# Slice 0 in other pieces: G in one transfer, X in halves, slice 1's X on the other queue, half of the narrow part in front of part B

## The chip, the cores and the metric

The kernel runs on one core of a Trainium2 chip. Times are device microseconds of that core; a timed execution is some 1.7 us longer than the span that the profile shows.

## The reference

The kernel computes the gradient of a weight: a sum over 16 batches and 512 rows of the product of an input (1024 columns) and an output gradient (768 columns).

```python
batch, m, k, n = 16, 512, 1024, 768
grad_weight = np.einsum('bmk,bmn->kn', input, grad_output)   # float32 in and out
```

As the kernel sees it, 8192 rows are 64 slices of 128; X is a slice of the input (128 x 1024), G one of the gradient (128 x 768).

## The kernel before

Matmuls run in bf16 and add up in fp32. Each slice takes 12 matmuls of 512 columns: part A (X groups 0 to 3 against the first 512 columns of G), part B (X groups 4 to 7 against the same), and part N (the last 256 columns of G, two interleaved sets, against each half of X). The list `ORDER` says up to which slice each part is taken in which turn; an exclamation mark closes the running sums of a part, which then leave their banks (the eight places in which matmuls add up).

Slices 1 to 63 come through GpSimd's queue, which casts to bf16 on the way (X of slice 1 excepted). Slice 0 and X of slice 1 come as fp32 through the sync and scalar queues, and are cast by DVE (VectorE) and ACT (ScalarE). While they come, TensorE runs matmuls on ones, to have its clock up by then. In the profiles PE is TensorE, PEld its weight load, POOL GpSimd and SP the sync engine.

```python
nc.sync.dma_start(out=gf[:, 0:NA], in_=G[0:P, 0:NA])      # NA = 512: 2 KB rows
nc.scalar.dma_start(out=xf[0], in_=X[0:P, :])             # 4 KB rows
nc.sync.dma_start(out=gf[:, NA:N], in_=G[0:P, NA:N])      # 1 KB rows
nc.scalar.dma_start(out=xf[1], in_=X[P : 2 * P, :])
# ... warm-up matmuls; loads of slices 1 to 63 on gpsimd ...
round_by("DVE", g0, gf, 0, 256)
round_by("ACT", g0, gf, 256, NA)
round_by("DVE", xs[0], xf[0], 0, P)
round_by("ACT", xs[0], xf[0], 2 * P, 4 * P)
round_by("DVE", xs[0], xf[0], P, 2 * P)
round_by("DVE", xs[0], xf[0], 4 * P, 6 * P)
round_by("ACT", xs[0], xf[0], 6 * P, 8 * P)
```

At the end, sums and stores of parts A and B alternate; the narrow part has been turned and stored before.

## Time and profile before

| | before |
|---|---|
| time, first three runs | 175.96 us (175.85 to 175.99) |
| span of the profile | 174.3 us |
| TensorE busy | 97% of the span |
| first useful matmul | 5.32 us |
| first matmul on slice 1 | 8.06 us |
| last matmul starts | 171.25 us |

The last three instants are start times in the trace. In its DMA records each of the first four transfers has 128 packets, one per row, and 16 semaphore writes, taken here as one for each of the 16 DMA engines; a transfer has landed when the semaphore is complete. The records do not name the engine; where the prediction speaks of the earliest one, it goes by the earliest semaphore write of each transfer. From 5.32 us on, matmuls of 512 columns follow each other at 0.216 us without a hole, so every shift at the head comes out at the end.

### The profile page before, as it was taken

How to read it: one execution, taken by the hardware profiler on the slowest of the kernel's cores; microseconds unless marked ns; L12 is line 12 of the kernel's file. 1: busy time of each engine (PE TensorE's matmuls, PEld its weight loads, DVE VectorE, ACT ScalarE, POOL GpSimd, SP SyncE). 2: the span in 40 equal slices, each digit the busy share in tenths (PEclk: the TensorE clock that was granted, in tenths of full speed). 3: DMA queues.
4: the chain of work that ended last, by engine and by line, in shares of the span. 5: the costliest groups of instructions: out<-in, count | busy, mean ns of one | idle time of the engine just before them, and what ended most of it. 6: DMA issues, size and time to landing. Idle time of an engine off the chain costs nothing.

```text
span 174.3 us, 2013 instructions
## 1 busy us (share of the span) xinstructions
PE 169.9 (97%) x793; PEld 78.4 (45%) x808; DVE 61.3 (35%) x103; ACT 6.2 (4%) x12; POOL 66.7 (38%) x129
## 2 busy tenths in 40 slices
PE   8999999999999999999999999999999999999993
PEld 3444444444444444444444444444444444444463
DVE  0655582883940039300000662200560003931122
ACT  2640000000000000000000000000000000000000
POOL 7444434444444444444444444444274200000000
PEclk9999999999999999999999999999999999999999
DMA  5999999999999999999999999999999990085623
GB/s 192 276 208 209 207 209 208 208 208 209 207 208 209 207 208 210 207 209 209 206 209 208 208 210 207 207 209 208 207 209 209 207 202 11 0 190 160 170 86 120
DMA packets 25048, 33.35 MB, mean 191 GB/s; under 512 B 6480, under 2 KB 16592, under 8 KB 25040
## 3 DMA queue, kind: packets, MB, share of 16 engines
q0 software_dynamic: 18000, 28.65, 89.9%
q10 hardware_dynamic: 4448, 2.10, 4.7%
q1 hardware_dynamic: 2592, 2.49, 4.2%
q8 instruction: 6, 0.10, 0.2%
q14 instruction: 2, 0.02, 0.0%
HBM read 58.72 MB, written 3.15 MB: 355 GB/s over the span
## 4 chain that ended last, share of the span: by engine, by line
PE 97%; issue 0%; DVE 0%
PE bank L127 63%; PE bank L134 32%; PE bank L81 3%; DVE acc L118 0%
## 5 line engine op out<-in xcount | busy, mean ns | idle before, releaser
L127 PE MATMUL bank<-gt,xt 128*128 128x512 bf16 (+2 forms) x515 | 108.3, 367 | 0.5
L127 PEld LDWEIGHTS <-xt 128*128 128x128 bf16 x524 | 50.2, 98 | 57.2
L118 DVE TENSOR_TENSOR acc<-bank,acc 128x512 f32<-128x512 f32 (+2 forms) x62 | 37.9, 667 | 73.4 <-PE bank L127 72.9
L134 PE MATMUL bank<-xt,gt 128*128 128x512 bf16 x242 | 54.8, 379 | 0.3
L97 POOL DMA_DIRECT2D xt<-in_input_dram x62 | 33.1, 533 | 38.7 <-DMA xt<-in_input_dram 36.5
L92 POOL DMA_DIRECT2D gt<-in_grad_output_dram x63 | 33.8, 536 | 31.2 <-DMA gt<-in_grad_output_dram 24.9
L134 PEld LDWEIGHTS <-gt 128*128 128x128 bf16 x252 | 24.6, 98 | 29.7
L118 DVE TENSOR_TENSOR acct<-bank,acct 128x512 f32<-128x512 f32 x24 | 15.7, 682 | 30.0 <-PE bank L134 29.9
L81 PE MATMUL bank<-const-bfloat16-1.0 128*128 128x512 bf16 (+1 forms) x12 | 4.6, 574 | 0.8 <-PEq L263 0.8
L81 PEld LDWEIGHTS <-const-bfloat16-1.0 128*128 128x128 bf16 x12 | 1.6, 140 | 3.5 <-issue 3.5
L122 DVE COPY acc<-bank 128x512 f32<-128x512 f32 x4 | 2.7, 687 | 1.0 <-PE bank L127 1.0
L180 DVE STREAM_TRANSPOSE turned<-acct 128x512 f32<-128x512 f32 x4 | 2.9, 715 | 0.1
L127 PEld LDWEIGHTS <-x 128*128 128x128 bf16 x16 | 1.6, 98 | 1.9 <-DVE x L107 0.2
L107 DVE CAST g<-gf 128x256 bf16<-128x256 f32 x2 | 0.6, 290 | 4.7 <-DMA gf<-in_grad_output_dram 4.7
L124 ACT COPY acc<-bank 128x512 f32<-128x512 f32 x4 | 2.1, 589 | 1.3 <-PE bank L127 1.3
L127 PE MATMUL bank<-gt,x 128*128 128x512 bf16 x8 | 2.1, 379 | 0.0
L127 PE MATMUL bank<-g,x 128*128 128x512 bf16 x8 | 2.0, 398 | 0.0
L122 DVE COPY acct<-bank 128x512 f32<-128x512 f32 x2 | 1.3, 686 | 1.3 <-PE bank L134 1.3
L107 ACT CAST x<-xf 128x256 bf16<-128x256 f32 x4 | 1.4, 409 | 0.0
L107 ACT ACT_TABLE_LOAD x1 | 1.3, 1283 | 1.7 <-PEq L263 1.7
L124 ACT COPY acct<-bank 128x512 f32<-128x512 f32 x2 | 1.1, 588 | 1.5 <-PE bank L134 1.5
L107 DVE CAST x<-xf 128x256 bf16<-128x256 f32 (+1 forms) x5 | 1.0, 260 | 0.0
(8 smaller groups left out, 3.3 us busy)
## 6 DMA issues: line engine op xcount, KB each, us to landing
xt<-in_input_dram POOLq DMA_DIRECT2D x62, 256.0 KB, 8.5
gt<-in_grad_output_dram POOLq DMA_DIRECT2D x63, 192.0 KB, 8.5
out_dram<-acc SPq DMA_DIRECT2D x13, 128.0 KB, 2.7
xf<-in_input_dram ACTq DMA_DIRECT2D x2, 512.0 KB, 5.1
out_dram<-turned ACTq DMA_DIRECT2D x4, 256.0 KB, 3.4
gf<-in_grad_output_dram SPq DMA_DIRECT2D x1, 256.0 KB, 3.9
out_dram<-acc SPq DMA_DIRECT2D x1, 256.0 KB, 2.0
gf<-in_grad_output_dram SPq DMA_DIRECT2D x1, 128.0 KB, 4.7
```

The costliest lines, as they stand in the source:

```text
L81: nc.tensor.matmul(wps[:, 0:cols], ones, nc.const_aps.tensor(1.0, (P, cols), bf16), start=True, stop=True,)
L92: nc.gpsimd.dma_start(out=gt, in_=G[s * P : (s + 1) * P, :])
L97: nc.gpsimd.dma_start(out=xs[s], in_=X[s * P : (s + 1) * P, :])
L107: copy(out=dst[:, c0:c1], in_=src[:, c0:c1])
L118: nc.vector.tensor_add(out=dst, in0=src, in1=dst)
L122: nc.vector.tensor_copy(out=dst, in_=src)
L124: nc.scalar.copy(out=dst, in_=src)
L127: nc.tensor.matmul(bank, xs[s][:, k * P : (k + 1) * P], gwide[s][:, c0:c1], start=start, stop=stop)
L134: nc.tensor.matmul(bank, gnarrow[s].rearrange("p (r t) -> p t r", t=NT)[:, t], xs[s][:, h * NA : (h + 1) * NA], start=start, stop=stop,)
L180: nc.vector.transpose(out=turned[:, h * hb : (h + 1) * hb, :, t], in_=dst.rearrange("p (b r) -> p b r", r=SQ),)
```

## The change

The intent: the first matmuls need only the first half of slice 0's X, so bring it alone and start earlier; bring G in larger rows; while the second half is on its way, do two of the four narrow matmuls (`H1`) first. The warm-up is shortened to match.

```diff
-    "A1! B1 N1 B2! N2 A2 N3! ...
+    "A1! H1 B1 N1 B2! N2 A2 N3! ...
-WARMUP = [512] * 10 + [128] * 2
+WARMUP = [512] * 9 + [128] * 4
@@ loads
-    nc.sync.dma_start(out=gf[:, 0:NA], in_=G[0:P, 0:NA])
-    nc.scalar.dma_start(out=xf[0], in_=X[0:P, :])
-    nc.sync.dma_start(out=gf[:, NA:N], in_=G[0:P, NA:N])
-    nc.scalar.dma_start(out=xf[1], in_=X[P : 2 * P, :])
+    nc.sync.dma_start(out=gf, in_=G[0:P, :])
+    nc.scalar.dma_start(out=xf[0][:, 0:NA], in_=X[0:P, 0:NA])
+    nc.sync.dma_start(out=xf[1], in_=X[P : 2 * P, :])
+    nc.scalar.dma_start(out=xf[0][:, NA:K], in_=X[0:P, NA:K])
@@ casts
-    round_by("DVE", g0, gf, 0, 256)
-    round_by("ACT", g0, gf, 256, NA)
-    ... (x of slice 0 in five casts)
+    round_by("DVE", g0, gf, 0, 304)
+    round_by("ACT", g0, gf, 304, NA)
+    for k in range(0, KS // 2, 2):
+        round_by("DVE", xs[0], xf[0], k * P, (k + 1) * P)
+        round_by("ACT", xs[0], xf[0], (k + 1) * P, (k + 2) * P)
+    round_by("DVE", g0, gf, NA, N)
@@ behind the copies of banks 0 and 1
-            if s == 0 and i == 0:
-                round_by("DVE", g0, gf, NA, N)
+            if s == 0 and i == 1:
+                round_by("DVE", xs[0], xf[0], 4 * P, 6 * P)
+                round_by("ACT", xs[0], xf[0], 6 * P, 8 * P)
... (half_slice(), which opens two banks of part N ahead, and its bookkeeping)
```

More of the change, by code (lines that the diff above doesn't have):

```diff
@@ L17 @@
 ORDER = (
-    "A1! B1 N1 B2! N2 A2 N3! A3 B3 A4! B5 N5 B6! N7 A6 N8! A9! B10 N9 B12! N12! A12! "
+    "A1! H1 B1 N1 B2! N2 A2 N3! A3 B3 A4! B5 N5 B6! N7 A6 N8! A9! B10 N9 B12! N12! A12! "
     "B15 AB17! n17! AB26! n26! AB41! n41! AB47 A50! B50! N64!"
 ).split()
-WARMUP = [512] * 10 + [128] * 2
+WARMUP = [512] * 9 + [128] * 4
 XBUFS = 42
@@ L107, in round_by @@
         copy(out=dst[:, c0:c1], in_=src[:, c0:c1])
-    round_by("DVE", g0, gf, 0, 256)
-    round_by("ACT", g0, gf, 256, NA)
-    round_by("DVE", xs[0], xf[0], 0, P)
-    round_by("ACT", xs[0], xf[0], 2 * P, 4 * P)
-    round_by("DVE", xs[0], xf[0], P, 2 * P)
-    round_by("DVE", xs[0], xf[0], 4 * P, 6 * P)
-    round_by("ACT", xs[0], xf[0], 6 * P, 8 * P)
+    round_by("DVE", g0, gf, 0, 304)
[4 more added lines that the diff above has]
+    round_by("DVE", g0, gf, NA, N)
     def add_out(dst, src):
@@ L148, in __init__ @@
             self.first = True
+            self.ahead = 0
             self.banks = {}
@@ L196, in slice_by_slice, with half_slice @@
                 part.done += 1
-                first = not part.banks
-                for i in range(len(part.groups)):
+                ahead, part.ahead = part.ahead, 0
+                first = len(part.banks) == ahead
+                for i in range(ahead, len(part.groups)):
                     if first:
                         open_bank(part, i)
-                for i in range(len(part.groups)):
+                for i in range(ahead, len(part.groups)):
                     add_slice(part, i, s, first, close and s == upto - 1)
+    def half_slice(part):
+        part.ahead = len(part.groups) // 2
+        for i in range(part.ahead):
+            open_bank(part, i)
+            add_slice(part, i, part.done, True, False)
     def bank_by_bank(part, upto):
@@ L212 @@
     for i, step in enumerate(ORDER):
-        if i == 2:
+        if step == "H1":
+            half_slice(parts["N"])
+            continue
+        if i == 3:
             round_by("DVE", xs[1], xf[1], 4 * P, 6 * P)
```

## The prediction

> **What bounds the kernel now.** I read the engine shares and the chain that ended last on the page first, then the chain in order of time, then the timeline of the first 9 us on PE, PEld, DVE and ACT, then the issues with their time to landing.
>
> ```profile
> PE 169.9 (97%) x793; PEld 78.4 (45%) x808; DVE 61.3 (35%) x103; ACT 6.2 (4%) x12; POOL 66.7 (38%) x129
> ...
> PE 97%; issue 0%; DVE 0%
> PE bank L127 63%; PE bank L134 32%; PE bank L81 3%; DVE acc L118 0%
> ```
>
> TensorE is the chain. In order of time it has no hole:
>
> ```profile
> 0.78 4.64 PE bank L81 x12
> 5.42 1.95 PE bank L127 x8
> 7.36 0.86 PE bank L134 x4
> 8.22 0.86 PE bank L127 x4
> ...
> 164.76 6.72 PE bank L127 x58
> ```
>
> The warm-up (L81) runs to 5.4 us, then useful matmuls follow start to start at 0.216 us (0.86 us for 4) until 171.5 us; the last sums and stores follow to 174.3 us. (The 0.05 us "issue" entries in this chain lie where a matmul's record is missing: two starts 0.43 us apart, twice the usual step.) So only two things can move the time: when the first useful matmul starts, and whether a hole opens. The first 9 us:
>
> ```profile
> 4.71 0.41 ACT L107 CAST g<-gf 128x256 bf16<-128x256 f32 x1 [1.76 <-DMA gf<-in_grad_output_dram]
> 4.71 0.29 DVE L107 CAST g<-gf 128x256 bf16<-128x256 f32 x1 [4.71 <-DMA gf<-in_grad_output_dram]
> ...
> 5.32 1.55 PEld L127 LDWEIGHTS <-x 128*128 128x128 bf16 x8 [0.17 <-DVE x L107]
> 5.32 2.04 PE L127 MATMUL bank<-g,x 128*128 128x512 bf16 x8
> ...
> 7.20 1.03 PE L134 MATMUL bank<-x,g 128*128 128x512 bf16 x4
> 8.06 1.03 PE L127 MATMUL bank<-gt,x 128*128 128x512 bf16 x4
> ```
>
> The first useful matmul starts at 5.32 us, 0.17 us after PEld was free, released by DVE's cast of x (5.04 to 5.27). That cast waited for X of slice 0, which landed at 5.02 us; G's wide part had landed at 4.68. The page has the times to landing (median us at the line's end; the landing instants come from the same trace):
>
> ```profile
> xf<-in_input_dram ACTq DMA_DIRECT2D x2, 512.0 KB, 5.1
> ...
> gf<-in_grad_output_dram SPq DMA_DIRECT2D x1, 256.0 KB, 3.9
> ...
> gf<-in_grad_output_dram SPq DMA_DIRECT2D x1, 128.0 KB, 4.7
> ```
>
> **What the Trainium skill says.** "TensorE: Matmul & The Clock Gate", Part 1: the array starts at half clock, and sustained activity opens the gate after about 3.4 us of a free-running window; 512 columns take 426.7 ns cold and 215.7 ns warm. The trace agrees: warm-up matmuls are 0.427 us apart, later ones 0.216, and the clock record begins at 5.63 us, inside the first useful matmul. "DMA: Bandwidth & Descriptors", "Queues, rings and completion order": each DMA engine takes packets of its queues in turn, and the semaphore write of a transfer lands behind that engine's earlier writes. The trace's packet records agree: on an engine, 2 KB packets of G and 4 KB packets of X alternate one to one. Both points carry the prediction.
>
> **The change part by part.**
>
> *Packets.* Typical durations in the records are 46 ns for 1 KB, 84 for 2 KB, 159 for 4 KB; 3 KB is not there, and I estimate 122 by the midpoint of 84 and 159. Each of the 16 engines carries 8 packets of each of the four first transfers. The engines repeat one pattern, the last lagging the first by 0.62 us. On the earliest one, before: first X packet 2.34; semaphore of G's wide part 3.68, of X slice 0 3.99; narrow G starts 4.00, X slice 1 4.25, so a queue pauses 0.25 to 0.3 us after its semaphore; semaphores 4.80 and 5.74. Landing is the latest engine's semaphore plus 0.3 to 0.4 us.
>
> *First phase after.* At the first X packet five G packets are left. 5 x 122 + 8 x 84 = 1.28 us instead of 5 x 84 + 8 x 159 = 1.69 (measured 1.65). With 0.06 us for the longer G packets before it, X's first half has its semaphore at 2.40 + 1.28 = 3.68 (0.31 earlier) and G at about 3.51 (0.17 earlier). Landings: X half 5.02 - 0.31 = 4.71, whole G 4.68 - 0.17 = 4.51.
>
> *First matmul.* DVE casts 304 columns: 0.29 us for 256 and 0.22 for 128 give 0.32, so 4.53 to 4.85; consecutive casts overlap by some 0.08, so x of group 0 runs 4.77 to 4.99, and with 0.055 us of release the weight load is at 5.05. ACT's shorter g cast is done by 4.9. The new warm-up (nine 512s and four 128s) ends at 0.78 + 9 x 0.427 + 4 x 0.107 = 5.05 instead of 5.26, so it is in nobody's way. The start moves 5.32 to 5.05. Until 5.63 the clock is half, so 0.27 us of earlier start is worth half: matmuls start at 5.05, 5.47, 5.77, 5.99, then the two narrow ones at 6.20 and 6.42, ready for part B at 6.63 against 6.77 for the seventh matmul before. Gain so far 0.13 us.
>
> *What part B waits for.* Before, groups 4 to 7 of slice 0 were in the same X transfer. Now they are in the second half, which shares every engine with the 4 KB rows of slice 1. On the earliest engine X slice 1 can start at 3.51 + 0.25 = 3.76 and both need 8 x (159 + 84) ns = 1.94 us, the half coming last: semaphore 5.70, nearly the 5.74 that X slice 1 had before, since the bytes in front are the same (1408 KB). That one landed at 7.03; so the half lands at about 6.99. DVE's copy of bank 0 (5.7 to 6.4) is then over; the cast of groups 4 and 5 takes 0.29: 7.01 to 7.30, and with 0.055 the first B matmul starts at 7.36. TensorE idles 7.36 - 6.63 = 0.73 us. The two narrow matmuls moved in front cover 2 x 0.216 = 0.43 of what would have been 1.16.
>
> *Afterwards.* Six matmuls later, at 7.36 + 6 x 0.216 = 8.66, comes slice 1 of B, against 8.06: 0.60 us late. X of slice 1 (landing about 7) is cast by DVE and ACT after their bank copies by 8.1; G of slice 1 landed at 7.49 before and may slip 0.1 or 0.2. Slice 2 landed at 8.46 and 9.70 for matmuls at 10.65, slice 3 at 10.65 and 11.90 for 13.2. A later TensorE only widens these margins. The moved g cast and the 304/208 split lie beside waiting time and cost nothing. The tail is untouched.
>
> *Sum.* -0.13 + 0.73 = +0.60 us: 176.56.
>
> **The rivals.**
>
> *The half lands in time.* If the smaller packets get ahead of the 4 KB ones, or slice 1 starts late, the half lands by 6.2 and its cast follows the bank copy at 6.3 to 6.6: no hole, 175.83. For it: the cast was put exactly behind that copy, as if the data were known to be there, and the warm-up shortened by 0.21 us fits my new start. Against it: strict alternation in the records. For a half-way landing at 6.6 the hole is 0.33 and the time 176.16.
>
> *The start does not move.* If G in 3 KB rows lands later instead (the first packets are slow), the start stays at 5.3 and the hole is about 0.5: 176.5 as well, for the end of the hole is set by the half's landing and not by the start. In that case moving G is worth nothing.
>
> *A larger loss.* If the idle time delayed the clock, or three queues share the engines while the half is in flight (the GpSimd queue sends its first packet at 5.28), the half lands at 7.3 and the time is 176.9. A throttle for microseconds would take more idle than 0.7 us by the skill's window, and I give it little.
>
> **Range and chances.** The mechanical sum says 176.56; the tuned look of the change speaks for the first rival, at about one in four. Between them I take 176.4, with 175.8 to 176.9 as the range: the low end is the gain without a hole, the high end a landing at 7.3. The three times before span 0.14 us. Two per cent would be 3.5 us, several times anything above.
>
> **What would show it.** In the timeline: the first cast of g near 4.5 instead of 4.71, the first L127 matmul near 5.05 instead of 5.32; six matmuls without a hole; then a PEld or PE idle entry of about 0.7 us released by DVE's cast of x; the first matmul on gt near 8.66 instead of 8.06; after it the same sequence, shifted. In the waits: DVE for xf at 6.4 to 7.0. Wrong if the second half lands before 6.3, if the start moves by less than 0.1, or if holes open after 9 us.

## The result

The changed kernel takes 177.36 us (median of 6 runs, 177.34 to 177.51) against 176.04 (6 runs, 175.85 to 176.47). A ratio is the mean time of one kernel's fast runs over that of the other's of the same rounds, so not quite the ratio of these medians: 1.0075, interval 1.0062 to 1.0087. It is slower by 1.3 us, which is outside the range that I gave (175.8 to 176.9).

The chain that ended last, on the page of the changed kernel:

```profile
PE 93%; DMA 4%; issue 1%; DVE 0%; ACTq 0%
PE bank L127 62%; PE bank L134 31%; DMA xf<-in_input_dram 4%; ACTq L74 0%; DVE x L108 0%; DVE acc L118 0%
```

A DMA has entered a chain that was all TensorE, and the warm-up's 3% is gone from it. In order of time (start us, duration us, what):

```profile
1.18 6.49 DMA xf<-in_input_dram
7.70 0.30 DVE x L108
8.05 1.04 PE bank L127 x4
...
166.05 6.72 PE bank L127 x58
```

Everything up to 8.05 us now hangs on one transfer, issued at 1.18 us on the scalar queue: the second half of slice 0's X, landing at 7.67 us. The last entry is 1.29 us later than before. The timeline of the changed kernel (start us, duration us, engine, line, operation, in brackets idle time and releaser):

```profile
4.58 0.32 DVE L108 CAST g<-gf 128x304 bf16<-128x304 f32 x1 [4.58 <-DMA gf<-in_grad_output_dram]
...
5.23 1.78 PE L127 MATMUL bank<-g,x 128*128 128x512 bf16 x4
...
6.84 0.60 PE L134 MATMUL bank<-x,g 128*128 128x512 bf16 x2
...
7.70 0.29 DVE L108 CAST x<-xf 128x256 bf16<-128x256 f32 x1 [1.13 <-DMA xf<-in_input_dram]
...
8.04 0.55 PEld L127 LDWEIGHTS <-x 128*128 128x128 bf16 x4 [1.10 <-DVE x L108]
8.05 1.04 PE L127 MATMUL bank<-g,x 128*128 128x512 bf16 x4 [0.61 <-DVE x L108]
...
9.36 0.59 PE L127 MATMUL bank<-gt,x 128*128 128x512 bf16 x2
```

The start did move, from 5.32 to 5.23 us. The four matmuls of part A take 1.78 us because most of them ran at half clock (starts 0.40 to 0.43 us apart; the clock record shows full clock only from 6.77 us, against 5.63 before). The two narrow ones start at 6.84 and 7.06, so part B could have started at 7.06 + 0.216 = 7.28. It starts at 8.05: a hole of 0.77 us. (The bracket's 0.61 is shorter because a matmul's end is modelled later than the next could start.) Slice 1 begins at 9.36 instead of 8.06, 1.29 us late, and the last matmul starts at 172.54 instead of 171.25, also 1.29 late. So nothing happens after 9 us, and the whole loss is 7.28 - 6.77 = 0.51 us of later matmuls in front, plus the 0.77 us hole.

Who had the engines while the second half was due? The DMA view of the window from 4.4 to 5.2 us, first of the kernel before (queue, kind: packets, MB, share of 16 engines):

```profile
q10 hardware_dynamic: 68, 0.27, 82.3%
q1 hardware_dynamic: 90, 0.08, 28.6%
```

and of the changed kernel:

```profile
q1 hardware_dynamic: 53, 0.22, 71.0%
q10 hardware_dynamic: 35, 0.06, 20.6%
```

Queue 1 is sync, queue 10 scalar. In the changed kernel sync carries slice 1's X here, which nobody needs yet, and scalar the tail of the first half and the beginning of the second: 53 packets of 4 KB against 35, of which 31 are rows of 2 KB and 4 semaphore writes. My prediction counted on one to one. In the next 0.8 us, from 5.2 to 6.0, it is one to one:

```profile
q1 hardware_dynamic: 47, 0.19, 59.4%
q10 hardware_dynamic: 47, 0.10, 30.8%
```

So the second half loses its time at the start. By the packet records slice 1's X began at 4.12 us, 0.31 after the earliest semaphore write of its queue's G, and the second half at 4.61, 0.61 after that of the first half. Meanwhile the engines moved less: 320 GB/s from 3.8 to 4.6 us, against 397 in the kernel before.

### The profile page after: what moved, and what is told of

It reads as the page before. It is cut to its first block, busy times and chain, and to the rows that moved or that the text cites. A ratio compares the mean times of both kernels' runs of the same rounds, so it can differ in the third digit from the quotient of the medians.

```text
span 175.6 us, 2016 instructions
## 1 busy us (share of the span) xinstructions
PE 170.6 (97%) x794; PEld 78.5 (45%) x809; DVE 61.4 (35%) x103; ACT 6.4 (4%) x13; POOL 66.4 (38%) x129
## 3 DMA queue, kind: packets, MB, share of 16 engines
q1 hardware_dynamic: 2592, 3.02, 5.0%
## 4 chain that ended last, share of the span: by engine, by line
PE 93%; DMA 4%; issue 1%; DVE 0%; ACTq 0%
PE bank L127 62%; PE bank L134 31%; DMA xf<-in_input_dram 4%; ACTq L74 0%; DVE x L108 0%; DVE acc L118 0%
## 5 line engine op out<-in xcount | busy, mean ns | idle before, releaser
L127 PE MATMUL bank<-g,x 128*128 128x512 bf16 x8 | 2.8, 491 | 0.6 <-DVE x L108 0.6
L108 DVE CAST g<-gf 128x304 bf16<-128x304 f32 (+1 forms) x2 | 0.6, 302 | 4.6 <-DMA gf<-in_grad_output_dram 4.6
L108 ACT CAST x<-xf 128x256 bf16<-128x256 f32 (+1 forms) x5 | 1.6, 361 | 0.8 <-DMA xf<-in_input_dram 0.8
L134 PE MATMUL bank<-x,g 128*128 128x512 bf16 x4 | 1.2, 379 | 0.0
```

The lines of the kernel that those rows point to most:

```text
L108: copy(out=dst[:, c0:c1], in_=src[:, c0:c1])
L127: nc.tensor.matmul(bank, xs[s][:, k * P : (k + 1) * P], gwide[s][:, c0:c1], start=start, stop=stop)
L134: nc.tensor.matmul(bank, gnarrow[s].rearrange("p (r t) -> p t r", t=NT)[:, t], xs[s][:, h * NA : (h + 1) * NA], start=start, stop=stop,)
```

## The experiments

Landings below are those of the trace, counted from the start of the span. The diffs start from the changed kernel, except where one says "before". By the 2% rule x1_held counts as "unclear" and all others as "same"; what is read here is smaller than 2% and rests on the intervals and the traces, one trace for each kernel.

### Slice 1's X last (x1_last)

```diff
-    nc.sync.dma_start(out=xf[1], in_=X[P : 2 * P, :])
     nc.scalar.dma_start(out=xf[0][:, NA:K], in_=X[0:P, NA:K])
+    nc.scalar.dma_start(out=xf[1], in_=X[P : 2 * P, :])
```

> The changed kernel, with X of slice 1 moved from the sync queue to the scalar queue behind the second half of slice 0's X, so nothing of its size shares the engines with that half. Theory (the hole in front of part B lasts until the second half lands, and the half is late because slice 1's 4 KB rows share the engines): the half lands near 6.0 us instead of 7.67, the hole of 0.77 us closes, first matmul on G of slice 1 at 8.0 (clock open at 5.6) to 8.6 (clock open at 6.8) instead of 9.36; time 175.9 to 176.6. Rival (small 2 KB rows land late by themselves): the half still lands after 7.2, hole stays, 177.2 to 177.4.

176.81 us, ratio to before 1.0041 (1.0026 to 1.0055). The second half landed at 5.50 us, and part B started at 6.78 without a hole: the theory's mechanism holds. But the time is above its range. Slice 1's X now landed at 8.63, because GpSimd's first transfers went in front of it (G of slice 1 landed at 6.64 instead of 7.49). The timeline on PE:

```profile
6.78 1.04 PE L127 MATMUL bank<-g,x 128*128 128x512 bf16 x4
7.65 0.59 PE L134 MATMUL bank<-x,g 128*128 128x512 bf16 x2
9.01 1.04 PE L127 MATMUL bank<-gt,x 128*128 128x512 bf16 x4 [0.76 <-DVE x L108]
```

The hole has moved from in front of part B to in front of slice 1.

### Without the narrow half in front (no_h1)

```diff
-    "A1! H1 B1 N1 ...
+    "A1! B1 N1 ...
```

> The changed kernel without the half of the narrow part in front of part B (all four narrow matmuls of slice 0 behind B). Theory (part B's start is set by a landing, not by the matmuls in front): B starts at the same 8.05 us, and two more matmuls follow it, so 0.43 us longer, 177.8. Rival (the new order of matmuls itself costs, by banks or casts): the same 177.36 or less.

177.72 us, ratio 1.0091 (1.0075 to 1.0107). Part B started at 8.03, as with H1, and the hole grew; the four narrow matmuls behind it put slice 1 at 9.77 instead of 9.36, 0.41 us later. So H1 pays for itself with its two matmuls, and a landing sets the start of part B.

### A longer warm-up (warm_11)

```diff
-WARMUP = [512] * 9 + [128] * 4
+WARMUP = [512] * 11 + [128] * 2
```

> The changed kernel with a longer warm-up, eleven of 512 and two of 128 columns, so that the first useful matmul comes at about 5.7 us instead of 5.23. Theory (the hole in front of part B absorbs everything before it): the same time within 0.1 us, 177.3 to 177.5, with B still starting near 8.05. Rival (an early start or the clock's opening decides): 0.2 to 0.5 us longer, or shorter if the longer warm-up opens the clock earlier.

177.36 us, ratio 1.0072 (1.0058 to 1.0086), the same as the changed kernel. The first useful matmul came at 5.63 instead of 5.23, part B at 8.04. An earlier start, the main purpose of the change, is worth nothing while the hole is there; nor does the clock matter: it rose at 6.08 in no_h1, at 6.50 here and at 6.77 in the changed kernel, and part B starts at 8.03 to 8.05 in all three.

### X of slice 0 in one piece again (whole_x0)

```diff
-    nc.scalar.dma_start(out=xf[0][:, 0:NA], in_=X[0:P, 0:NA])
+    nc.scalar.dma_start(out=xf[0], in_=X[0:P, :])
-    nc.scalar.dma_start(out=xf[0][:, NA:K], in_=X[0:P, NA:K])
```

> The changed kernel with slice 0's X in one transfer of whole rows again, G in one transfer and X of slice 1 on the sync queue as changed. Theory (cutting X in halves puts slice 1's rows in front of the second half): X of slice 0 lands near 5.3 to 5.4, first matmul near 5.7, no hole; time 176.1 to 176.8, depending on when the clock opens. Rival (G in one transfer or slice 1 on the sync queue is what costs): 177.2 or more.

176.46 us, ratio 1.0022 (1.0008 to 1.0036). X landed at 5.38, the first matmul started at 5.71, no hole. Cutting X in halves is what makes the hole possible. What is left, some 0.4 us in the medians, fits the later start (5.71 against 5.32), for G in one piece delays X.

### G in two pieces again (g_split)

```diff
-    nc.sync.dma_start(out=gf, in_=G[0:P, :])
+    nc.sync.dma_start(out=gf[:, 0:NA], in_=G[0:P, 0:NA])
+    nc.sync.dma_start(out=gf[:, NA:N], in_=G[0:P, NA:N])
```

> The changed kernel with only G of slice 0 back in two transfers (wide, then narrow) on the sync queue, X of slice 1 behind them, X of slice 0 still in halves. Theory (X of slice 1 reaches the engines as soon as the whole G is through, just before the second half starts, and takes two packets for its one): now the 1 KB narrow rows stand in that place, the half lands at 5.6 to 6.3 us, no hole in front of part B; slice 1's X lands 7.2 to 7.7; time 175.9 to 176.5. Rival (any second half on the scalar queue is late while slice 1 shares the engines): half after 7.2, 177.0 or more.

177.37 us, ratio 1.0072 (1.0059 to 1.0084): the time missed the expectation, though the landing that it is about hit it. The second half landed at 5.40 with the narrow rows of G in the place of slice 1's X. Then slice 1's X landed at 8.44 instead of by 7.7, and slice 1 began at 8.82, 0.76 us late. The rest is at the end, and was not expected: from the start of the last matmul to the end of the span took 3.44 us instead of 3.03. With five transfers at the head instead of four, the rotation of the eight semaphores puts the last store on the first of them. The end of the program waits for the eight in a fixed order, 0.06 us each; here the other waits come after the last store has landed, where before they came while it was under way. I read this from the semaphore waits in the trace. No run was made for it alone, but x1_halves, also with five, has 3.45 us, and lead, with five and one store fewer, 3.02.

### The two second transfers exchanged (swap)

```diff
-    nc.sync.dma_start(out=xf[1], in_=X[P : 2 * P, :])
-    nc.scalar.dma_start(out=xf[0][:, NA:K], in_=X[0:P, NA:K])
+    nc.sync.dma_start(out=xf[0][:, NA:K], in_=X[0:P, NA:K])
+    nc.scalar.dma_start(out=xf[1], in_=X[P : 2 * P, :])
```

> The changed kernel with the two second transfers exchanged: second half of slice 0's X behind G on sync, X of slice 1 behind the first half on scalar. Theory (who starts second on the engines loses): the half lands at 6.6 to 7.0 instead of 7.67, part B starts 7.0 to 7.4 instead of 8.05, time 176.4 to 176.8. Rival (2 KB packets always lose two to one against 4 KB packets, whichever queue): half after 7.4, time 177.1 or more.

176.19 us, ratio 1.0008 (0.9996 to 1.0021): as fast as before, 0.2 us better than expected. The half landed at 6.27 and slice 1's X at 7.44; there is no hole. The DMA view of the same window as above, 4.4 to 5.2 us:

```profile
q10 hardware_dynamic: 51, 0.21, 65.8%
q1 hardware_dynamic: 66, 0.13, 42.2%
```

The half, now on queue 1, has the 66, so rows of 2 KB do not always lose to rows of 4 KB. The bytes are those of the changed kernel, and all of slice 1's X lands only 0.25 us later than there (7.19). The useful start at 5.00 us brought no gain in this trace, for its clock rose only at 6.78; slice 1 began at 8.47, and the profiled run is the slowest of the five (176.44).

### Slice 1's X in halves too (x1_halves)

```diff
-    nc.sync.dma_start(out=xf[1], in_=X[P : 2 * P, :])
+    nc.sync.dma_start(out=xf[1][:, NA:K], in_=X[P : 2 * P, NA:K])
     nc.scalar.dma_start(out=xf[0][:, NA:K], in_=X[0:P, NA:K])
+    nc.scalar.dma_start(out=xf[1][:, 0:NA], in_=X[P : 2 * P, 0:NA])
```

> The changed kernel with X of slice 1 in halves too: the half that part B needs first behind G on sync, the other behind slice 0's second half on scalar. Theory (the bytes that share the engines with slice 0's second half decide): 256 KB less in front, the half lands at 6.2 to 6.7, part B starts no later than 7.1 to 7.3, slice 1's last half lands at 7.3 to 7.8; time 176.0 to 176.6. Rival: as x1_last, a later landing takes the place of the first and the time stays near 176.8.

176.96 us, ratio 1.0058 (1.0045 to 1.0070), above the expectation. The second half landed at 6.88, part B started at 7.25, slice 1 at 8.56, 0.50 us late; the longer end adds 0.42. With 256 KB less in front, the half still came later than the 256 KB of slice 1 on the sync queue (6.27): fewer bytes help less than coming first.

### The short warm-up alone (b_warm9)

```diff
 before:
-WARMUP = [512] * 10 + [128] * 2
+WARMUP = [512] * 9 + [128] * 4
```

> The kernel before with nothing changed but the warm-up, nine of 512 and four of 128 columns. Theory (the clock opens at an instant that varies from run to run, and the first useful matmul waits for slice 0's X): the same as before within 0.2 us, 175.85 to 176.25, first matmul at 5.3. Rival (the shorter warm-up itself opens the clock a microsecond later, as in the changed kernel's trace): 0.3 to 0.5 us longer in every run.

175.98 us, ratio 1.0004 (0.9990 to 1.0017). The first matmul started at 5.28, and the clock was up at 3.78 us already. With the same nine-and-four warm-up the clock record began at 6.77 in the changed kernel's profile, 6.08 in no_h1 and 4.90 in x1_last. So the instant is not set by this warm-up; it varies from trace to trace.

### The sync queue held back by 0.2 us (g_late)

```diff
+    nc.vector.memset(gf[:, 0:64], 0.0)
     nc.sync.dma_start(out=gf, in_=G[0:P, :])
     ...
+    nc.vector.memset(xf[1][:, 0:64], 0.0)
     nc.sync.dma_start(out=xf[1], in_=X[P : 2 * P, :])
```

> The changed kernel with two small DVE memsets (64 columns of the tiles of G and of slice 1's X, overwritten by the transfers) that hold the sync queue back by some 0.2 us, so that the scalar queue starts first and its first half is through before G. Theory (of two queues, the one whose next transfer comes to the engines first is served first): slice 0's second half now comes first, lands 6.2 to 6.8 instead of 7.67, slice 1's X after it, part B starts by 7.2, time 176.2 to 176.8. Rival (the engines prefer the sync queue, whoever comes first): the half lands at 7.4 or later, time 177.1 or more.

Four runs: 176.06, 176.14, 176.38 and 177.38; median 176.26, ratio 1.0022, interval 0.9991 to 1.0054, so the time alone does not tell it from the kernel before. The trace tells more. G was issued at 0.96 instead of 0.74 us. The first half landed at 3.80 (4.92 in the changed kernel), the second at 5.52, slice 1's X at 7.37, and there is no hole. The window from 4.2 to 5.0 us:

```profile
q10 hardware_dynamic: 126, 0.23, 75.7%
q1 hardware_dynamic: 34, 0.10, 32.2%
```

The scalar queue, which had the smaller count in the changed kernel, has 126 packets against 34 (semaphore writes included). So it is not the sync queue that is preferred. The second half began at 4.06 us, slice 1's X only at 4.71, when three quarters of the half's packets had started: here the one that came first was mostly on its way before the other began. The run at 177.38 has the time of the changed kernel; that the order fell the other way there would fit, but it has no trace.

### What is needed next in front (lead)

```diff
-    nc.sync.dma_start(out=gf, in_=G[0:P, :])
+    nc.sync.dma_start(out=gf[:, 0:NA], in_=G[0:P, 0:NA])
     nc.scalar.dma_start(out=xf[0][:, 0:NA], in_=X[0:P, 0:NA])
-    nc.sync.dma_start(out=xf[1], in_=X[P : 2 * P, :])
-    nc.scalar.dma_start(out=xf[0][:, NA:K], in_=X[0:P, NA:K])
+    nc.sync.dma_start(out=xf[0][:, NA:K], in_=X[0:P, NA:K])
+    nc.sync.dma_start(out=gf[:, NA:N], in_=G[0:P, NA:N])
+    nc.scalar.dma_start(out=xf[1], in_=X[P : 2 * P, :])
... (no H1; warm-up 8 and 4; narrow cast behind X's; one store fewer)
```

> An attempt to beat both: only what a matmul group needs next is in front. Sync: wide G, second half of slice 0's X, narrow G; scalar: first half, X of slice 1; order of matmuls as before; warm-up eight of 512 and four of 128; one store fewer at the end, so that the number of transfers and with it the order of the final waits is as before. Theory: first half lands 4.2 to 4.4, first matmul near 4.7 instead of 5.3, second half 5.7 to 6.2, slice 1 by 7.5, no hole over 0.3 us; 175.7 to 176.1, the clock's instant deciding. Rival (what is put last lands late and opens a hole in its turn): slice 1 or narrow G after 8, time 176.4 or more.

177.41 us, ratio 1.0068 (1.0055 to 1.0080): a miss. The first half landed at 4.58, the second at 5.91, slice 1's X at 6.85, and the narrow part of G, last on its queue beside GpSimd's transfers, at 8.04. The timeline on PE:

```profile
4.89 2.63 PE L127 MATMUL bank<-g,x 128*128 128x512 bf16 x8
8.41 1.19 PE L134 MATMUL bank<-x,g 128*128 128x512 bf16 x4 [0.89 <-DVE g L109]
```

The rival came true: what is put last opens a hole of its own.

### Slice 1's X issued 2 us later (x1_held)

```diff
-    nc.sync.dma_start(out=xf[1], in_=X[P : 2 * P, :])
     nc.scalar.dma_start(out=xf[0][:, NA:K], in_=X[0:P, NA:K])
+    nc.scalar.copy(out=xf[1][:, 0:64], in_=nc.const_aps.tensor(1.0, (P, 64), bf16))
+    nc.sync.dma_start(out=xf[1], in_=X[P : 2 * P, :])
```

> The changed kernel with nothing moved but the instant at which slice 1's X is issued: a small ACT copy into its tile, after ACT's table load, holds that one transfer back from 1.2 to about 3.2 us. G, both halves and their queues stay. Theory (slice 1's X delays slice 0's second half only because it comes to the engines first): the second half lands at 5.5 to 6.3 instead of 7.67, slice 1's X at 7.3 to 8.0, no hole over 0.3 us in front of part B; time 175.8 to 176.4. Rival (G in one transfer, or the half's own queue, makes it late): half after 7, time 177.0 or more.

179.44 us, ratio 1.0201 (1.0161 to 1.0241), runs near 178.5 and near 180.4. The part that the theory is about held: the second half landed at 5.73 and part B started at 7.08. The time did not. In order of time:

```profile
3.23 6.92 DMA xf<-in_input_dram
...
10.18 0.31 DVE x L109
...
10.53 1.04 PE bank L128 x4
```

Issued at 3.23, slice 1's X landed at 10.15. By the packet records none of it had arrived by 6.8 us, while GpSimd's queue moved 230 between 4.8 and 6.8. The two groups of times go with the granted clock: 0.988 to 0.990 in the three longer runs, 0.998 to 1.000 in the shorter. One per cent of 178 us is about 2 us (an estimate), as much as lies between the groups. Why the clock was lower there is open; the profiled run belongs to the shorter group, and its slice 1, 2.47 us late, accounts for that group alone.

## Why the prediction was wrong

**What bounds, and where to look: right.** The loss sits in front of slice 1, and from there the matmuls follow without a hole. By my own list, though, the start should have moved by at least 0.1 us; it moved by 0.09.

**First phase after: wrong, 0.3 us.** I had the semaphores of the earliest engine at 3.51 (G) and 3.68 (first half); they came at 3.82 and 4.01. Before, X in 4 KB rows had its own at 3.99. 128 KB less in the first two transfers did not bring the first half forward there, nor on the latest engine (4.63 against 4.61 before); the landing came 0.1 us earlier (4.92 against 5.02) only because it followed that semaphore sooner. In the other kernels with the same first two transfers, untouched in issue, the half landed anywhere from 4.59 (x1_halves) to 5.23 (x1_held), so such an estimate is no better than 0.3 us.

**First matmul: right in direction, a third of the size.** 0.09 us earlier instead of 0.27. It did not matter, as warm_11 shows.

**Clock at 5.63: an assumption that does not hold.** It came at 6.77 in this trace, so part B could have started at 7.28 and not at 6.63. The hole hid this.

**What part B waits for: the mechanism right, the size wrong; this is the step that failed.** The half was last, its landing set the start of part B, and H1 covered two matmuls of it (no_h1). But I let slice 1's X and the half alternate one to one from the start and put the half's semaphore at 5.70 on the earliest engine. It came at 6.45, 0.75 us later. 0.33 of it is from the first phase. The other 0.42 is not a matter of shares alone, for in my sum the half comes last whatever the shares are. The sum took it that each queue goes on 0.25 to 0.3 us after its semaphore, that the engines are then never idle, and that the same 1408 KB in front take the same time as before. The traces show otherwise: the second half began 0.61 us after the first half's earliest semaphore, and from 3.8 to 4.6 us the engines moved 320 GB/s. The two other traces with the same four transfers in the same order agree (no_h1 310, warm_11 320); before it was 397, and in swap and g_late, where the half comes first, 389. At the rate of before that is some 0.15 us of work (an estimate: 0.8 us x 77 of 397). From 5.4 us on GpSimd's queue took part too, with 64 of the 140 packets from 6.0 to 6.8. How the 0.42 divides between these, no run separates. The landing was 7.67 instead of 6.99, part B 8.05 instead of 7.36, and that difference of 0.69 us is the whole miss at slice 1 (1.29 late instead of 0.60). Swap and g_late settle that coming second is the cause: with the same bytes in the same four transfers, the half lands at 6.27 or 5.52 as soon as it comes first, and both kernels are back within noise of the one before. What makes the later transfer begin late, no run tells.

**Rivals.** The half in time: wrong, by 1.5 us. The start does not move: nearly so, and worth as little as said. A larger loss: the right direction. Of its two reasons, the clock did come late but did not matter (warm_11), and GpSimd's queue is not the whole of it, since the half was behind already at 5.2 us, when that queue had moved nothing. My choice of 176.4, below my own sum of 176.56, leaned on how tuned the change looked; that was no evidence.

**Sum.** Predicted -0.13 + 0.73 = +0.60; measured +0.51 and +0.77, +1.29 in the trace (the last digit by rounding) and 1.3 in the times.

## What to carry to other kernels

When several transfers race at the head of a kernel, look at who arrives first, and do not count on an even share of the engines: here a transfer that nobody needed yet was the first to follow, and the one that was needed landed 1.4 us later than with the two exchanged (7.67 against 6.27). Cutting a transfer to start sooner puts its second piece in the race; if something less urgent comes in front of it, the gain at the start is lost in a hole two steps later. No rearrangement beat the kernel before. In x1_last, g_split, lead and x1_held what was put last came late beside the loads of the following slices; in x1_halves the second half itself was still late (6.88), and the end longer. Swap and g_late, which let the second half come first, only drew level.

## What the Trainium skill lacked or had wrong

- "DMA: Bandwidth & Descriptors", "Queues, rings and completion order", has the engines take turns between their queues, packet by packet. For two transfers that are both running the traces agree (X and G of slice 0, 3.0 to 3.6 us before: 41 and 43 records), if a record of the trace, one row, is taken for such a packet; the page lets a packet hold many descriptors. It lacks what happens when a transfer comes new to engines that another is using. After its queue's earliest semaphore write the second half began 0.61 us later in the changed kernel, slice 1's X 0.65 us later in g_late, against 0.31 for slice 1's X in the changed kernel, which came first. In x1_held nothing arrived by 6.8 us of a transfer issued at 3.23, while another queue moved 230 packets.
- "TensorE: Matmul & The Clock Gate", Part 1, gives about 4 us to full clock with 500 ns of variation from run to run; further down it warns that the window runs freely and that one kernel showed 6, 11 or 14 slow matmuls. With warm-up matmuls from 0.78 us on in every kernel, the clock record began between 3.69 us (whole_x0) and 6.78 us (swap), so 2.9 to 6.0 us after the first matmul, or 7 to 14 warm-up matmuls of 0.427 us. 500 ns is too narrow; the wider statement fits.
- I found no page on the order of the final waits. In g_split and x1_halves, with five head transfers instead of four, the time from the last matmul's start to the end was 3.44 and 3.45 us instead of 3.03, because the last store stood on the first of eight semaphores that are waited for in a fixed order.
